# Attention kept in the order of issue on all engines, with each step of a head released by an account of when its operands are ready

## The chip, the cores and the metric

The kernel runs on one core of one Trainium2 chip. The metric is the device time of one execution in microseconds (us). A core has a matrix engine (PE, with its weight loads shown as PEld), a vector engine (DVE), a scalar engine (ACT), a general engine (POOL) and a queue that issues transfers (SP). Each engine works through its own queue in order and waits at an instruction until that instruction's operands are there.

## The reference, cut to what matters

Two layers on 256 tokens of width 1024, in float32. Each layer is a gated feed-forward part, a mixer, and a second feed-forward part. The mixer of layer 0 is differential attention, that of layer 1 is retention. The change touches the attention:

```python
q, k, v = jnp.split(xn @ w_in, 3, axis=-1)            # 8 heads, 2 maps of 64, values of 128
q = _rms(q.reshape(B, T, H, 2, Dh), q_gain) * (Dh ** -0.5)
k = _rms(k.reshape(B, T, H, 2, Dh), k_gain)
...
s = jnp.einsum('bhmqd,bhmkd->bhmqk', qb, k)           # causal, with a slope per head
p = jax.nn.softmax(s + bias[None, :, None], axis=-1)
a = p[:, :, 0] - lmbda * p[:, :, 1]
o = jnp.einsum('bhqk,bhkd->bhqd', a, v)
...
o = _rms(o, subln) * (1.0 - lam_init)
return o.reshape(B, T, H * 2 * Dh) @ w_out
```

## The kernel before, in words

**Products.** Each float32 weight matrix is split into two parts that PE takes at full rate: `hi`, a rounded copy made by ACT, and `lo = raw - hi`, made by DVE. A product is three matmuls of 128 x 512: hi by hi, lo by hi, hi by lo. The class `Weights` loads raw blocks (`load`, six buffers), rounds them (`round`, `remain`) into at most four parts ahead of PE, and hands them out in a planned order (`take`). One part of a projection serves 24 wide matmuls.

**The account.** `Flow` carries an account of time while the program is written out: `flow.now` moves with every matmul (`mm` calls `tick`), and `flow.free` says until when DVE and ACT are taken. `Timed` wraps DVE and ACT and charges every instruction a fixed price and one per column (160 ns and 1.04 ns for DVE, 190 and 0.85 for ACT). Side work is written as generators: `spawn` starts one, `yield n` asks to go on n ns later, and `tick` resumes those that are due. What DVE and ACT have left is given to rounding weights (`paced`).

**The order.** By default a scheduler of the framework, which has its own idea of when an instruction is ready, may put the instructions of an engine in another order than they were issued in. `keep_order` adds an order between successive instructions of each engine. `order_from_here` marks where a kept stretch begins and `order_to_here` closes it. Before the change, stretches are kept from the start to the first `q` projection of attention, from the last chunks of attention's output projection to the first value projection of retention, and from the last chunks of retention's output projection to the end. Between them the scheduler's order holds, but for SP, whose order is kept over the whole program.

**Attention.** `proj_tokens` projects `q`, `k` of heads 0 to 3 (group 0), then of heads 4 to 7 (group 1), into PSUM banks `pj`. `grouped_norm` squares them (`sq`, ACT), sums (`ss`, DVE), takes the power -1/2 (`r`, POOL), scales (`qn`, DVE) and transposes (`ptn`, PE); ACT copies the result to `T_q` or `T_k`. `head` makes for each of its two maps the scores `s` (PE), adds the bias (`sb`, DVE), takes the negative maximum (`nm`, DVE) and the exponential with its sum (`p` and `z`, ACT); then the reciprocal of the sums (`rz`) and the difference of the maps (`att`, DVE), its transposes (`pa`, PE) and their copy (`aT`, ACT). `values` multiplies with `v` into `po`, and `values_norm` norms that into `oT`. The values of both groups are projected after `k` of group 1, and then the output projection `y_dao` runs: two chunks of 24 wide matmuls each that need `oT` of group 0, and two that need group 1. `ffn` is the feed-forward part; its `finish_unit` transposes a gated unit `g` into `hT` through a bank `ptg`.

Of the kernel before, what the change touches and what calls it, by code (L numbers as in the profile page):

```python
# [21 lines left out]
NT = T // P  # L22
# [38 lines left out]
class Flow:  # L61
# [7 lines left out]
    def __init__(self):  # L69
        self.now, self.tasks, self.n = 0.0, [], 0  # L70
        self.urgent, self.casts, self.idle = 0, 0, lambda: None
        self.free = {"DVE": 0.0, "ACT": 0.0}

# [41 lines left out]

    def soon(self, at, by=0):
        return at <= self.now + self.SOON + by


class Timed:  # L120
# [5 lines left out]
    def __getattr__(self, name):  # L126
        issue = getattr(self.engine, name)

        def call(*args, **kw):
            n = max(math.prod(x.shape[1:]) for x in args if hasattr(x, "shape"))  # L130
            self.flow.charge(self.key, self.fixed + self.each * n)
# [220 lines left out]
def trunk_kernel(ctx: ExitStack, tc: tile.TileContext, io, out: bass.AP):  # L352
# [9 lines left out]
    flow = Flow()  # L362
# [119 lines left out]
    def transposes(name, src, n):  # L482
# [3 lines left out]
        flow.now += 115 * n  # L486
        return pt
# [52 lines left out]
    def inv_rms(ss_ap, n, name):  # L540
        r = small.tile([P, n], F32, tag=f"r{n}", name=f"r_{name}")
        nc.gpsimd.tensor_tensor(r, ss_ap, half[:, :n], ALU.pow)
        return r
# [118 lines left out]
    def out_proj(nk, src, coef, name, gain, sums=None):  # L662
# [3 lines left out]
        order_from_here()  # L666
# [7 lines left out]
    def ffn(name, before, sums, next_gain, next_sums=None, last=False):  # L674
# [13 lines left out]
        def finish_unit(j, gs):  # L688
            yield max(g[1] for g in gs) - flow.now + 500
# [9 lines left out]
            split_to(hT[j][:, :, 0, :], hT[j][:, :, 1, :], pt.rearrange("p (i c) -> p i c", c=T))  # L699
            ends[j] = flow.free["DVE"]  # L700
# [117 lines left out]
    def attention(before, next_gain, next_sums):  # L818
# [3 lines left out]
        def grouped_norm(ps, ng, dim, name, margin):  # L822
# [3 lines left out]
            flow.behind("DVE", flow.free["ACT"])  # L826
# [4 lines left out]
            yield flow.through("DVE") + (1900 if ng == 8 else 1200)  # L831
# [7 lines left out]
            yield flow.through("DVE") + margin  # L839
# [23 lines left out]
        def head(g, hh, qT, kT, need, wait, res):  # L863

            yield wait
            yield from all_of(need)
            while flow.through("DVE") > 1500:
                yield 300
            slope = 2.0 ** (-8.0 * (g * 4 + hh + 1) / DA_H)
            z = small.tile([P, 4], F32, tag="z", name=f"z_{g}{hh}")  # L870
            ps_ = []
            for m in range(2):
                name = f"{g}{hh}{m}"
# [8 lines left out]
                flow.now += 650  # L882
                sb = work.tile([P, 384], F32, tag="a", name=f"sb_{name}")
# [3 lines left out]
                for t, cs in enumerate(sides):  # L887
                    vec.tensor_reduce(nm[:, t : t + 1], sb[:, cs], AX.X, ALU.max, negate=True)
                    sca.activation(
# [7 lines left out]
                flow.behind("DVE", flow.free["ACT"] - 700)  # L897
            yield flow.through("DVE", "ACT")
# [11 lines left out]
            yield flow.through("DVE") + 1500  # L910
            pt = transposes(f"pa_{g}{hh}", a, 3)
            if (g, hh // 2) not in res:
                res[g, hh // 2] = blk(f"aT_{g}{hh}", F32, [2, 384])
            sca.copy(res[g, hh // 2][:, hh % 2, :], pt[:, :384])
# [3 lines left out]
        def values(g, v, need, outs):  # L918

            po = [bank(f"po_{g}{t}") for t in range(NT)]  # L920
            for hh in range(4):
                yield from all_of([need[hh]])
                if hh == 0:
# [260 lines left out]
```

## Time and profile before

| | |
|---|---|
| median of three runs | 1066.44 us (1064.53 to 1068.25) |
| the profiled execution | 1065.27 us, its span 1063.5 us |
| PE busy | 1045.8 us, 98% |
| DVE busy | 780.6 us, 73% |
| ACT busy | 589.1 us, 55% |
| POOL busy | 52.2 us, 5% |
| read from memory | 184 GB/s over the span |

The profile is one execution of the program. The span runs from its first to its last instruction; the rest of its time lies around it. A busy time is the sum of an engine's records without overlaps. Records of successive matmuls overlap, so for PE the distance between starts says more than the length of a record. A note such as `[0.40 <-DVE att L132]` says that the engine stood idle for 0.40 us before the instruction and which instruction's end released it. `PEclk` is the share of full clock granted to PE.

### The profile page before, as it was taken

The page shows a single profiled execution, that of the slowest core. Times are in us where ns is not written, and L with a number is a line of the kernel's source. Part 1 is how long each engine was busy: PE and PEld are TensorE (multiplying, and loading weights), DVE is VectorE, ACT ScalarE, POOL GpSimd, SP SyncE. Part 2 cuts the span into 40 slices and gives each one's busy share as a digit, 9 for nine tenths or more (in the row PEclk, how much of TensorE's full clock was granted, in tenths as well). Part 3 has the DMA queues.
Part 4 walks back from the last instruction along what each step waited for, and adds up shares of the span by engine and source line. Part 5 has one row for each costly group of instructions (what it writes and reads, how often), then busy time and mean ns, then how long its engine had stood idle before and what let it go on. Part 6 is the DMA issues. An engine that isn't in the chain of part 4 may idle for free.

```text
span 1063.5 us, 12519 instructions
## 1 busy us (share of the span) xinstructions
PE 1045.8 (98%) x4883; PEld 859.6 (81%) x4883; DVE 780.6 (73%) x751; ACT 589.1 (55%) x657; POOL 52.2 (5%) x62
## 2 busy tenths in 40 slices
PE   8999999999899999999999999999999999999998
PEld 6787888877578888888888888888888888888886
DVE  6687888688767878787787778666556547877883
ACT  7464565656546655655656456555444436565651
POOL 0000000121001000000000000000000000000000
PEclk9999999999899999999999999999999999999999
DMA  9967968364138697869578867664454497597741
GB/s 285 320 202 227 297 203 307 112 242 152 41 118 238 187 268 234 241 237 266 150 238 237 238 214 268 228 232 142 136 166 168 148 283 202 189 265 234 223 159 39
DMA packets 138814, 221.61 MB, mean 208 GB/s; under 512 B 5762, under 2 KB 104834, under 8 KB 135683
## 3 DMA queue, kind: packets, MB, share of 16 engines
q1 hardware_dynamic: 135298, 195.65, 54.8%
q0 software_dynamic: 3456, 25.17, 12.3%
q8 instruction: 38, 0.62, 0.2%
q14 instruction: 22, 0.17, 0.0%
HBM read 194.58 MB, written 1.05 MB: 184 GB/s over the span
## 4 chain that ended last, share of the span: by engine, by line
PE 84%; DMA 5%; DVE 5%; issue 2%; ACT 2%; SPq 1%; POOL 1%; POOLq 0%; DVEq 0%; ACTq 0%
PE b_f L445 19%; PE ps_f L445 16%; PE pj L445 11%; PE y_f1o L445 6%; PE y_f2o L445 6%; PE y_f3o L445 6%; PE pqk L445 4%; PE y_f0o L445 4%; PE y_rto L445 4%; DMA raw<-raw 3%; DVE lo L132 2%; DMA raw<-in_ffn_w_in_dram 2%; PE y_dao L445 2%; PE ptg_f L694 2%; ACT hi L132 1%
## 5 line engine op out<-in xcount | busy, mean ns | idle before, releaser
L132 DVE TENSOR_TENSOR lo<-raw,hi 128x2048 fp32r<-128x2048 f32 (+2 forms) x224 | 491.6, 2211 | 110.1 <-ACT hi L132 108.4
L132 ACT CAST hi<-raw 128x2048 fp32r<-128x2048 f32 (+2 forms) x224 | 412.7, 1851 | 198.0 <-DVE raw L132 99.6
L445 PE MATMUL pj<-hi,xn_f2o 128*128 128x512 f32 x256 | 80.9, 393 | 0.0
L445 PE MATMUL pj<-hi,xn_f0o 128*128 128x512 f32 x192 | 62.3, 402 | 0.0
L445 PEld LDWEIGHTS pj<-hi,xn_f2o 128*128 128x128 f32 x256 | 48.0, 188 | 9.6
L445 PE MATMUL y_f1o<-hi,hT_f 128*128 128x512 f32 x176 | 55.6, 392 | 0.0
L445 PE MATMUL y_f2o<-hi,hT_f 128*128 128x512 f32 x176 | 55.6, 392 | 0.0
L445 PE MATMUL y_f0o<-hi,hT_f 128*128 128x512 f32 x176 | 55.3, 392 | 0.0
L445 PE MATMUL y_f3o<-hi,hT_f 128*128 128x512 f32 x176 | 55.3, 392 | 0.0
L132 DVE TENSOR_TENSOR raw<-raw,raw 128x2048 f32<-128x2048 f32 x24 | 54.8, 2283 | 0.0
L445 PE MATMUL ps_f<-hi,xn_in 128*128 128x512 f32 x160 | 50.6, 394 | 1.1 <-ACT xn_in L132 0.9
L445 PE MATMUL ps_f<-hi,xn_dao 128*128 128x512 f32 x160 | 50.2, 393 | 0.0
L445 PE MATMUL ps_f<-hi,xn_rto 128*128 128x512 f32 x160 | 50.2, 393 | 0.0
L445 PE MATMUL ps_f<-hi,xn_f1o 128*128 128x512 f32 x160 | 50.2, 393 | 0.0
L445 PE MATMUL pj<-lo,xn_f2o 128*128 128x512 f32 x128 | 50.1, 392 | 0.0
L232 POOL DMA_DIRECT2D raw<-raw x24 | 21.0, 876 | 494.7 <-DMA raw<-in_ffn_w_in_dram 302.3
L445 PE MATMUL pqk<-xn_f2o,hi 128*128 128x512 f32 x128 | 44.5, 397 | 0.0
L132 DVE TENSOR_TENSOR hT_f<-ptg_f,hT_f 128x512 fp32r<-128x512 f32 x44 | 30.2, 686 | 19.2 <-ACT hT_f L132 18.8
L445 PEld LDWEIGHTS pj<-hi,xn_f0o 128*128 128x128 f32 x192 | 36.4, 192 | 8.0 <-issue 1.0
L445 PE MATMUL y_rto<-hi,mT 128*128 128x512 f32 x128 | 39.7, 390 | 0.0
L445 PE MATMUL pj<-lo,xn_f0o 128*128 128x512 f32 x96 | 38.7, 403 | 0.0
L445 PEld LDWEIGHTS y_f0o<-hi,hT_f 128*128 128x128 f32 x176 | 33.1, 188 | 6.8
(281 smaller groups left out, 2037.3 us busy)
## 6 DMA issues: line engine op xcount, KB each, us to landing
raw<-in_ffn_w_in_dram SPq DMA_DIRECT2D x168, 512.0 KB, 5.6
raw<-in_ffn_w_out_dram SPq DMA_DIRECT2D x44, 1024.0 KB, 6.6
raw<-raw POOLq DMA_DIRECT2D x24, 1024.0 KB, 8.2
raw<-in_rt_w_in_dram SPq DMA_DIRECT2D x24, 1024.0 KB, 5.9
raw<-in_da_w_in_dram SPq DMA_DIRECT2D x12, 1024.0 KB, 6.1
raw<-in_rt_w_out_dram SPq DMA_DIRECT2D x8, 1024.0 KB, 5.1
raw<-in_da_w_out_dram SPq DMA_DIRECT2D x4, 1024.0 KB, 5.0
raw<-in_ffn_w_in_dram SPq DMA_DIRECT2D x16, 128.0 KB, 3.7
```

The source lines that it names most:

```text
L132: return issue(*args, **kw)
L232: self.nc.gpsimd.dma_start(self.raws[to], self.raws[by], accum_op=ALU.add)
L445: nc.tensor.matmul(ps, lhsT=lhsT, rhs=rhs, start=start, stop=stop, skip_group_check=more)
L694: nc.tensor.transpose(pt[:, at : at + P], gs[t][0][:, i * P : (i + 1) * P], ident)
```

## The change

Attention is put into a kept stretch: `order_to_here` after its first projection goes, and `order_from_here` before the last chunks of an output projection is left only for retention's (`rto`). One stretch now runs from the start to retention's first value projection.

The account learns when each tile is ready. `Timed` moves an engine's account behind the tiles that an instruction reads, notes the end for the tile that it writes, and charges 190 ns more where a sum is accumulated. Transposes, scores and powers note their results too. `flow.until(x)` is the time until x is ready, less 50 ns.

The steps of `grouped_norm`, `head` and `values` yield until their operands are ready, in place of fixed margins. A head begins its scores when the head before has handed out its exponentials (`over`), where before it was started 3000 ns after it, and it begins each map only while DVE has no more than 1200 ns queued. In every feed-forward part `finish_unit` keeps the pacer from rounding weights on ACT in the last 1500 ns before its transposes.

```diff
--- before.py
+++ after.py
@@ -70,6 +70,7 @@
         self.now, self.tasks, self.n = 0.0, [], 0
         self.urgent, self.casts, self.idle = 0, 0, lambda: None
         self.free = {"DVE": 0.0, "ACT": 0.0}
+        self.ready = {}
 
     def spawn(self, gen):
         task = {"gen": gen, "due": self.now, "done": False, "n": self.n}
@@ -113,6 +114,14 @@
 
         return max(0, max(self.free[e] for e in engines) - self.now)
 
+    def made(self, x, at):
+
+        self.ready[x.tensor.name] = at
+
+    def until(self, *xs):
+
+        return max(0, max(self.ready.get(x.tensor.name, 0) for x in xs) - self.now - 50)
+
     def soon(self, at, by=0):
         return at <= self.now + self.SOON + by
 
@@ -127,8 +136,17 @@
         issue = getattr(self.engine, name)
 
         def call(*args, **kw):
-            n = max(math.prod(x.shape[1:]) for x in args if hasattr(x, "shape"))
-            self.flow.charge(self.key, self.fixed + self.each * n)
+            flow = self.flow
+            tiles = [x for x in args if hasattr(x, "tensor")]
+            n = max(math.prod(x.shape[1:]) for x in tiles)
+            reads = tiles[1:] + [x for k, x in kw.items() if hasattr(x, "tensor")]
+            flow.behind(self.key, max([flow.ready.get(x.tensor.name, 0) for x in reads] + [0]))
+            flow.charge(self.key, self.fixed + self.each * n)
+            end = flow.free[self.key]
+            flow.made(tiles[0], end)
+            if "accum_out" in kw:
+                flow.charge(self.key, 190)
+                flow.made(kw["accum_out"], flow.free[self.key])
             return issue(*args, **kw)
 
         return call
@@ -484,6 +502,7 @@
         for j in range(n):
             nc.tensor.transpose(pt[:, j * P : (j + 1) * P], src[:, j * P : (j + 1) * P], ident)
         flow.now += 115 * n
+        flow.made(pt, flow.now + 150)
         return pt
 
     def normed(task, t):
@@ -540,6 +559,7 @@
     def inv_rms(ss_ap, n, name):
         r = small.tile([P, n], F32, tag=f"r{n}", name=f"r_{name}")
         nc.gpsimd.tensor_tensor(r, ss_ap, half[:, :n], ALU.pow)
+        flow.made(r, max(flow.now, flow.ready.get(ss_ap.tensor.name, 0)) + (800, 1200, 1900)[n // 4])
         return r
 
     def new_xn(name):
@@ -663,7 +683,8 @@
         y = OutProj(nk, src, coef, name, gain, sums=sums)
         for c in range(nk // 2 - TAIL):
             y.chunk(c)
-        order_from_here()
+        if name == "rto":
+            order_from_here()
         return y.finish()
 
 
@@ -686,7 +707,10 @@
             return g, flow.free["DVE"]
 
         def finish_unit(j, gs):
-            yield max(g[1] for g in gs) - flow.now + 500
+            wait = max(g[1] for g in gs) - flow.now + 500
+            yield max(0, wait - 1500)
+            flow.casts += 1
+            yield min(wait, 1500)
             pt = bank(f"ptg_{name}{j}")
             for i in range(2):
                 for t in range(NT):
@@ -697,6 +721,7 @@
             flow.now += 300
             hT[j] = blk(f"hT_{name}{j}", F32R, [2, 2, T])
             split_to(hT[j][:, :, 0, :], hT[j][:, :, 1, :], pt.rearrange("p (i c) -> p i c", c=T))
+            flow.casts -= 1
             ends[j] = flow.free["DVE"]
 
         def unit(*js):
@@ -823,12 +848,12 @@
 
             sq = work.tile([P, 512], F32, tag="xs", name=f"sq_{name}", bufs=3)
             sca.activation(sq, ps, AF.Square)
-            flow.behind("DVE", flow.free["ACT"])
+            yield flow.until(sq)
             ss = small.tile([P, ng], F32, tag=f"ss{ng}", name=f"ss_{name}")
             vec.tensor_reduce(ss, sq.rearrange("p (g d) -> p g d", d=dim), AX.X, ALU.add)
             vec.tensor_scalar_add(ss, ss, dim * EPS)
             r = inv_rms(ss, ng, name)
-            yield flow.through("DVE") + (1900 if ng == 8 else 1200)
+            yield flow.until(r)
             qn = work.tile([P, 512], F32, tag="xs", name=f"qn_{name}", bufs=3)
             vec.tensor_tensor(
                 qn.rearrange("p (g d) -> p g d", d=dim),
@@ -836,7 +861,7 @@
                 r.unsqueeze(2).broadcast_to([P, ng, dim]),
                 ALU.mult,
             )
-            yield flow.through("DVE") + margin
+            yield flow.until(qn) + 100
             return transposes(f"ptn_{name}", qn, 4).rearrange("p (j c) -> p j c", c=P)
 
         def heads_norm(t, ps, dst, gcol, name):
@@ -860,16 +885,19 @@
 
         sides = (slice(0, P), slice(P, 384))
 
-        def head(g, hh, qT, kT, need, wait, res):
-
-            yield wait
+        def head(g, hh, qT, kT, need, wait, state, res):
+
+            yield 0
             yield from all_of(need)
-            while flow.through("DVE") > 1500:
-                yield 300
+            while wait is not None and not wait["over"]:
+                yield 200
             slope = 2.0 ** (-8.0 * (g * 4 + hh + 1) / DA_H)
             z = small.tile([P, 4], F32, tag="z", name=f"z_{g}{hh}")
+            yield flow.until(qT, kT)
             ps_ = []
             for m in range(2):
+                while flow.through("DVE") > 1200:
+                    yield 200
                 name = f"{g}{hh}{m}"
                 ms = slice(m * DH, (m + 1) * DH)
                 ps = bank(f"s_{name}")
@@ -880,12 +908,16 @@
                     ps[:, P:384], lhsT=qT[ms, hh, P:T], rhs=kT[ms, hh, :], start=True, stop=True
                 )
                 flow.now += 650
+                flow.made(ps, flow.now + 100)
+                yield flow.until(ps)
                 sb = work.tile([P, 384], F32, tag="a", name=f"sb_{name}")
                 vec.scalar_tensor_tensor(sb, dist, -slope, ps[:, :384], ALU.mult, ALU.add)
                 nm = small.tile([P, 2], F32, tag="nm", name=f"nm_{name}")
                 p = work.tile([P, 384], F32, tag="sb"[m], name=f"p_{name}")
                 for t, cs in enumerate(sides):
                     vec.tensor_reduce(nm[:, t : t + 1], sb[:, cs], AX.X, ALU.max, negate=True)
+                yield flow.until(nm) - 300
+                for t, cs in enumerate(sides):
                     sca.activation(
                         p[:, cs],
                         sb[:, cs],
@@ -894,8 +926,8 @@
                         accum_out=z[:, 2 * m + t : 2 * m + t + 1],
                     )
                 ps_.append(p)
-                flow.behind("DVE", flow.free["ACT"] - 700)
-            yield flow.through("DVE", "ACT")
+            state["over"] = True
+            yield flow.until(z)
             rz = small.tile([P, 4], F32, tag="rz", name=f"rz_{g}{hh}")
             vec.reciprocal(rz, z)
             vec.tensor_scalar(rz[:, 2:4], rz[:, 2:4], nlam, None, ALU.mult)
@@ -907,10 +939,11 @@
                 vec.scalar_tensor_tensor(
                     a[:, cs], ps_[0][:, cs], rz[:, t : t + 1], ps_[1][:, cs], ALU.mult, ALU.add
                 )
-            yield flow.through("DVE") + 1500
+            yield flow.until(a) + 150
             pt = transposes(f"pa_{g}{hh}", a, 3)
             if (g, hh // 2) not in res:
                 res[g, hh // 2] = blk(f"aT_{g}{hh}", F32, [2, 384])
+            yield flow.until(pt)
             sca.copy(res[g, hh // 2][:, hh % 2, :], pt[:, :384])
 
         aTs, oT = {}, {}
@@ -920,8 +953,7 @@
             po = [bank(f"po_{g}{t}") for t in range(NT)]
             for hh in range(4):
                 yield from all_of([need[hh]])
-                if hh == 0:
-                    yield flow.through("ACT") + 1000
+                yield flow.until(aTs[g, hh // 2], v) + 100
                 aT = aTs[g, hh // 2][:, hh % 2, :]
                 hs = slice(hh * P, (hh + 1) * P)
                 for t, cs, vt, first, last in (
@@ -934,9 +966,10 @@
                     )
                 flow.now += 670
                 yield 0
+            for t in range(NT):
+                flow.made(po[t], flow.now + 100)
             norms = [flow.spawn(values_norm(g, t, po[t], outs)) for t in range(NT)]
-            yield 0
-            flow.join(*norms)
+            yield from all_of(norms)
 
         def values_norm(g, t, po, outs):
             pt = yield from grouped_norm(po, 4, 2 * DH, f"o{g}{t}", (2500, 500)[g])
@@ -946,7 +979,7 @@
             flow.behind("DVE", flow.free["ACT"])
             vec.scalar_tensor_tensor(lo, pt, go, hi, ALU.mult, ALU.subtract)
 
-        heads = {}
+        heads, states = {}, []
         wts.reserve(2)
         for g in range(2):
             qT, need = proj_heads(gq, f"q{g}", before if g == 0 else (None, None))
@@ -955,12 +988,15 @@
                 vec.tensor_scalar(
                     nlam, le[:, 1:2], le[:, 0:1], LAM_INIT, ALU.subtract, ALU.subtract
                 )
-                order_to_here()
             kT, more = proj_heads(gk, f"k{g}")
             need += more
-            heads[g] = [
-                flow.spawn(head(g, hh, qT, kT, need, 3000 * hh, aTs)) for hh in range(4)
-            ]
+            heads[g] = []
+            for hh in range(4):
+                states.append({"over": False})
+                wait = states[-2] if len(states) > 1 else None
+                heads[g].append(
+                    flow.spawn(head(g, hh, qT, kT, list(need), wait, states[-1], aTs))
+                )
         tv = []
         for g in range(2):
             v = blk(f"v_{g}", F32, [NT, 512])
```

## Rows read from the trace of the kernel before

**Rows 1.** Windows: length, then PE, PEld, DVE, ACT, POOL busy, PEclk, DMA, GB/s
```profile
0.00:100.00 100.00, 93.25 (x414) 74.13 (x415) 71.18 (x75) 60.24 (x70) 5.83 (x12) 1.00 0.91 272
198.40:323.20 124.80, 118.18 (x586) 93.21 (x585) 92.92 (x170) 72.11 (x132) 21.11 (x15) 0.96 0.41 133
271.20:290.50 19.30, 14.36 (x62) 9.99 (x61) 14.85 (x46) 9.91 (x36) 2.01 (x2) 0.74 0.13 43
340.00:1000.00 660.00, 659.99 (x3089) 548.42 (x3089) 483.54 (x400) 362.18 (x364) 22.44 (x31) 1.00 0.71 218
```

**Rows 2.** Chain of work that ended last: start us, length us, what
```profile
258.74 0.43 PE s L876 x4
...
305.16 15.68 PE y_dao L445 x69
```

**Rows 3.** Windows of PE's `pj` (two) and `y_dao` (one) alone, as rows 1
```profile
271.20:290.50 19.30, 7.92 (x26) 0.74 0.13 43
277.00:295.40 18.40, 7.54 (x24) 0.72 0.00 0
...
295.30:304.90 9.60, 5.20 (x20) 1.00 0.39 111
```

**Rows 4.** Timeline of PE: start us, length us, line, instruction, idle before and releaser
```profile
257.54 0.30 PE L485 MATMUL pa<-ident,att 128*128 128x128 f32 x1 [0.59 <-DVE att L132]
...
275.70 0.30 PE L485 MATMUL pa<-ident,att 128*128 128x128 f32 x1 [0.40 <-DVE att L132]
...
278.71 0.30 PE L485 MATMUL pa<-ident,att 128*128 128x128 f32 x1 [1.78 <-DVE att L132]
...
287.68 0.45 PE L485 MATMUL pa<-ident,att 128*128 128x128 f32 x1 [2.76 <-DVE att L132]
...
303.53 0.66 PE L485 MATMUL ptn_o<-ident,qn_o 128*128 128x128 f32 x4 [0.99 <-DVE qn_o L132]
```

**Rows 5.** Timeline of DVE in attention, columns as rows 4
```profile
232.86 1.01 DVE L132 SCALAR_TENSOR_TENSOR sb<-dist,s 128x384 f32<-128x384 f32 x2
...
258.44 0.69 DVE L132 TENSOR_TENSOR qn_k<-pj,r_k 128x512 f32<-128x512 f32 x1 [0.65 <-POOL r_k L542]
259.63 0.56 DVE L132 SCALAR_TENSOR_TENSOR sb<-dist,s 128x384 f32<-128x384 f32 x1 [0.50 <-PE s L879]
...
262.66 0.18 DVE L132 RECIPROCAL rz<-z 128x4 f32<-128x4 f32 x1 [0.72 <-ACT p L132]
...
263.60 0.74 DVE L132 SCALAR_TENSOR_TENSOR att<-p,rz,p 128x128 f32<-128x128 f32 x2
...
287.85 1.12 DVE L132 TENSOR_REDUCE nm<-sb 128x1 f32<-128x128 f32 x4
...
294.17 2.29 DVE L132 TENSOR_TENSOR lo<-raw,hi 128x2048 fp32r<-128x2048 f32 x1 [2.37 <-ACT hi L132]
...
305.92 0.75 DVE L132 SCALAR_TENSOR_TENSOR oT<-ptn_o,go,oT 128x512 fp32r<-128x512 f32 x1 [0.22 <-ACT oT L132]
```

**Rows 6.** Tile `ptg_f`, 0 to 100 us and whole: idle before it, us, times
```profile
  DVE g_f L132: 6.7, 4
```

**Rows 7.** Timeline of ACT in attention, columns as rows 4
```profile
230.68 0.69 ACT L132 ACTIVATE T_k<-ptn_k,gk 128x512 f32<-128x512 f32 x1 [1.67 <-PE ptn_k L485]
...
266.21 0.67 ACT L132 ACTIVATE T_k<-ptn_k,gk 128x512 f32<-128x512 f32 x1
...
294.04 0.47 ACT L132 COPY aT<-pa 128x384 f32<-128x384 f32 x1
...
299.68 0.60 ACT L132 ACTIVATE sq_o<-po 128x512 f32<-128x512 f32 x1 [1.98 <-PE po L932]
```

**Rows 8.** Waits of PE and PEld, 198 to 324 us: us in total, times, longest
```profile
PE pa L485 <- DVE att L132: 5.5, 4, 2.8
...
PEld pa L485 <- issue: 7.3, 6, 3.5
...
PEld pa L485 <- ACT v L132: 1.0, 1, 1.0
```

## The prediction, made before the change was run

> **What bounds the kernel now.** I read the page first: TensorE (PE) is busy for 98% of the span. That share is too coarse here, because a matmul's record covers more than its slot, so I cut the span into stages [rows 1]. From 340 to 1000 us PE is never idle, while DVE has 27% and ACT 45% to spare. There the kernel is bound by PE alone, and an edit that only moves DVE or ACT work can gain nothing. The attention stage, 198.4 to 323.2 us, is different: in 271.2 to 290.5 us PE shows 14.36 us of 19.30, the DMA engines stand almost still (0.13), and the mean granted clock is 0.74, so part of the stretch ran at 1.2 instead of 2.4 GHz after PE had stood idle in it [rows 1].
>
> What a stretch should have cost I take from two prices: 69 wide matmuls in a row took 15.68 us, so 0.227 us each, and four records of a head's scores took 0.43 us, so 0.108 us each [rows 2]. In 271.2 to 290.5 us there are 62 PE records [rows 1], 26 of them wide [rows 3]: 26 x 0.227 + 36 x 0.108 = 9.8 us; some eight changes between narrow and wide matmuls cost about 0.1 us each, so 10.6 us. Lost: 8.7 us. The timeline of PE shows where: before the transposes `pa` at 275.70, 278.71 and 287.68 [rows 4]. All three wait for `att` from DVE, and wide matmuls stand right behind them in the queue: 24 of `v1`'s start only after 277 [rows 3], 48 more belong to the first two chunks of `y_dao`, and only those after them need the second group of heads. So PE waits with 72 x 0.227 = 16 us of work behind the wait that does not need it. That is a fault of order, not of speed. The same at 303.53, where `ptn_o` stands in front of `y_dao` (0.99 us) [rows 4], and at 257.54, where PE stood 0.59 us. Together 8.7 + 1.0 + 0.6 = **10.3 us**: no ordering of attention can give more than that.
>
> **The change part by part.** *Order of issue kept on all engines in attention* (two marks moved). It adds and removes no instruction. It gives the queue its order from the kernel's own account, not from the scheduler's. The account holds PE to a step of 7 + 512/2.4 = 220 ns against 227 measured [rows 2], and charges a head's DVE steps more than they take: `sb` 160 + 1.04 x 384 = 559 ns against 1.01 us for two [rows 5]. So a product of DVE is as a rule ready before the place in PE's queue that was given to its reader. I take the 10.3 us back in full, and charge for what this order can lose:
>
> *Gates.* Twelve norms, eight `att`, sixteen score steps and eight heads of `values` are now handed out 100 to 150 ns after (or up to 50 ns before) the account has the operand: 44 gates on PE, with everything queued behind each. The nearest row is the 44 groups `ptg_f`, gated with 500 ns: PE stood before them four times, 6.7 us, all within the first 100 us [rows 6], where the DMA share was 0.91 [rows 1]; after that it never waited for their operand. Bounds: 0 and 6.7 us. The DMA share in attention is far below that [rows 1], nearer to the later groups, but the margins are a third of theirs: I take 2 us. The old gates had 500 to 2500 ns more; these are what the shorter chain pays with.
>
> *Chain of the heads.* A head's scores now begin when the one before has its exponentials handed out (`over`), and the second map's after the first's. A head whose scores met no weight work took from 258.7 us to the reciprocal at 262.66, 4.0 us [rows 2, 5]. To this come parts of the last head's `rz` to `att` that do not fit into gaps (about 0.7 of the 1.7 us from 262.66 to 264.34 [rows 5]), and the `lo` of the weights, 2.29 us each [rows 5], one per 24 wide matmuls, so one in about 7 us with the narrow ones. T = 4.0 + 0.7 + 2.29 x T/7 gives T = 7.0 us per head. The first starts at 231.4 (end of `T_k` [rows 7]). The first of group 1 needs `T_k` of `k1`: `qn_k` ended at 259.1 [rows 5], the copy of its transposes came only at 266.21 [rows 7]; gated at 100 ns they give `T_k` at about 262, and four heads end at 290. Before, it took from 288.7 (300 ns ahead of the last maximum) to 294.5 until the last `aT` [rows 5, 7]: 5.8 us. The last head's six narrow records of `po` take 6 x 0.108 = 0.7, the norm from `sq_o` at 299.68 to the end of `oT` at 306.67 took 7.0 for two halves [rows 5, 7], of which the first is enough to go on, so 6.5, and 0.3 for the poll: 7.5. End: 290 + 5.8 + 7.5 = 303.3 us.
>
> PE needs that `oT` at its 49th `y_dao`. Before, 20 of them were done at 304.9 [rows 3], so it came there at 304.9 + 28 x 0.227 = 311.3; with 10.3 us given back, at 301.0. So a stall of 2.3 us remains, and this is what is late next: DVE's chain of the last heads. Each 0.1 us on T costs 0.4 to 0.8 us once this cover is gone.
>
> *Accounts* (`made`, `until`, reads in `Timed`, 190 ns for an accumulator's read). They also move weight work in the feed-forward parts. Cover: PE without a gap from 340 us on [rows 1]. If it were gone, the four waits of 6.7 us [rows 6] are what could move, 1.7 us each; I take 0, and as ends one of them gone or added, -2 and +2 us.
>
> *`finish_unit` holds casts back for 1.5 us* before its transposes, 44 times. Hidden by ACT's idle 40% and by up to four parts rounded ahead; without the cover each could make a part 1.5 us late, and nothing shows a part late from 340 us on. Taken at 0. A gain is excluded there, since PE has no gap to give back.
>
> *Queues passed.* SP's order was kept over the whole kernel already. On POOL only the twelve powers `r_q`, `r_k` and `r_o` stand in this stage, each behind its own `ss`, and in the order in which their readers want them. Neither costs.
>
> Sum: -10.3 + 2 (gates) + 2.3 (chain) = -6 us. The profiled execution took 1065.27 us (span 1063.5 and 1.8 around it); it becomes 1059.3. The median of the three runs shown is 1.2 us above it: **1060.4 us**.
>
> **The rivals.**
> 1. *The chain is covered in full.* If the DVE steps, which are shorter than their charges, let T come to 6.4 us or less, `oT` is ready by 301 and only gates remain: -8 to -10.3, about 1057 us. For it: two `sb` are charged 1.12 us and take 1.01, and the small reductions are charged 160 ns each on top of their columns. Against it: a `lo` that slips in costs 2.29 us whatever the charges [rows 5].
> 2. *The chain becomes the bound, and the kernel slower.* Price: in group 0 before, the first `sb` of heads 0 and 3 stand 26.8 us apart, 8.9 us per head [rows 5]. If the new order keeps that spacing, the end comes at 231.4 + 8 x 8.9 + 13.3 = 315.9, a stall of 14.9 us: with the gates' 2, less the 10.3, +6.6, so about 1073 us. It decides from 231.4 + 8T + 13.3 = 309.3, T = 8.1 us: two `lo` in each head instead of one (4.7 + 4.6 = 9.3) do it. Against it: the new code waits for the scores of the head before alone, and lets its `rz` to `att` run beside the next scores.
> 3. *The waits at `pa` are not the order's.* If a `pa` waited for a PSUM bank, the order of issue leaves it as it is, and 0 to 2 us come back: 1065 us. The trace has 1.0 us before `pa` that ACT's copy of `v` ended, which reads another bank; 5.5 us on PE are `att`'s own, and 7.3 us of the weight loads before `pa` have no cause named [rows 8]. The Trainium skill, Perfetto Trace Analysis, section Identifying Performance Opportunities, says that the same gap repeated on the engine that should be full can mean too few buffers for the next tile; by that rule this case, and not the order, would be the whole story. The trace agrees for 1.0 us of it and not for the 5.5.
>
> **How the numbers follow.** A difference of less than 0.3%, 3.2 us, cannot be told from no change. Forecast (-3.2 to -8): 0.48. Rival 1 (-8 to -12.3): 0.17. Rival 3, or a chain with T near 8 (within 3.2 us): 0.18. Rival 2: 0.17. So faster 0.65, same 0.18, slower 0.17. The range goes from all 10.3 us with the accounts' 2 (1066.4 - 12.3 = 1054) to 1069, a little above no change, which leaves out the larger part of rival 2.
>
> **What would show it.** PE in 271 to 290 us with no gap over 0.5 us before `pa`, and granted clock 1.00 there; `y_dao` ending near 317 instead of 323 us; the one wait left before the 49th `y_dao`, for `oT`; spacing of the heads' first `sb` near 7 us. A spacing over 8.1, or a wait of more than 8 us before `oT`'s first reader, makes the forecast wrong. New gaps in 340 to 1000 us would mean that the accounts or the held casts cost what I took at 0.

## The result and the profile after

The changed kernel takes 1074.80 us in the median against 1066.67 for the kernel before, 1.0069 times as long (95% interval 1.0052 to 1.0087). The forecast was 1060.4, in a range of 1054 to 1069. It was wrong in sign; rival 2, the chain of the heads as the bound, had 1073. That this lies near is in part luck: rival 2 had a stall of 14.9 us and nothing for the scores, and the trace has 12.0 and 6.6.

The profiled execution has a span of 1071.6 us, 8.1 more than before. By the start of the first `pj`, the end of the last `y_dao` and the end of the last `y_f3o` in both traces it divides so: up to attention -1.4 us (198.4 before, 197.0 after), attention +7.5 (124.9 before, 132.4 after), behind it +2.0 (736.1 before, 738.1 after).

The windows of the kernel after answer [rows 1] (columns: stretch, its length, then busy time and count of PE, PEld, DVE, ACT and POOL, granted clock of PE, DMA share, GB/s):

```profile
198.40:323.20 124.80, 117.95 (x551) 90.18 (x550) 92.47 (x162) 68.72 (x125) 22.48 (x14) 0.95 0.41 131
271.20:290.50 19.30, 19.30 (x103) 15.22 (x102) 15.55 (x31) 11.48 (x26) 1.98 (x2) 1.00 0.18 56
340.00:1000.00 660.00, 658.73 (x3078) 545.89 (x3077) 483.91 (x400) 362.59 (x366) 21.61 (x30) 1.00 0.70 216
```

The stretch that held the forecast's gain, 271.2 to 290.5 us, is now full: 19.30 of 19.30 us and clock 1.00, where before it was 14.36 and 0.74. The waits of [rows 4] before `pa` are gone. They came back in another place. PE's timeline of the kernel after, end of attention (start, length, operation; in brackets the idle time just before it and who ended it):

```profile
302.05 0.59 PE L907 MATMUL s<-T_k,T_q 64*128 64x256 f32 x2
302.58 0.55 PE L503 MATMUL pa<-ident,att 128*128 128x128 f32 x3
303.94 0.94 PE L964 MATMUL po<-v,aT 128*128 128x128 f32 x6 [0.81 <-ACT aT L150]
307.29 0.45 PE L503 MATMUL pa<-ident,att 128*128 128x128 f32 x1 [2.42 <-DVE att L150]
307.98 0.69 PE L503 MATMUL pa<-ident,att 128*128 128x128 f32 x2 [0.25 <-DVE att L150]
309.24 1.65 PE L964 MATMUL po<-v,aT 128*128 128x128 f32 x6 [0.57 <-ACT aT L150]
313.49 2.10 PE L503 MATMUL ptn_o<-ident,qn_o 128*128 128x128 f32 x8 [2.60 <-DVE qn_o L150]
315.44 1.58 PE L463 MATMUL y_dao<-hi,oT 128*128 128x512 f32 x2
316.82 0.63 PE L463 MATMUL y_dao<-lo,oT 128*128 128x512 f32 x1
317.25 1.05 PE L463 MATMUL y_dao<-hi,oT 128*128 128x512 f32 x2
318.11 0.63 PE L463 MATMUL y_dao<-lo,oT 128*128 128x512 f32 x1
318.53 0.85 PE L463 MATMUL y_dao<-hi,oT 128*128 128x512 f32 x2
319.23 0.39 PE L463 MATMUL y_dao<-lo,oT 128*128 128x512 f32 x1
```

From 302.58 to 315.44 PE does 26 narrow matmuls, 2.8 us at 0.108 each, in 12.9: 10.0 us lost. Of these 6.65 are idle time, the five notes in brackets added up; the other 3.4 are narrow matmuls that took longer than their price, most of them at the lower clock. No wide matmul stands between, since all 336 that don't need the second group (288 `pj`, 48 `y_dao`) were issued ahead of the last head's second scores. Then eight wide matmuls, 315.44 to 319.23, take 3.8 us instead of 8 x 0.227 = 1.8: 2.0 more, at the lower clock. This tail costs 12 us.

Why the last head is so late, DVE's timeline of the kernel after shows; it answers [rows 5]. The first two rows are the first `sb` of the first head and of the fifth, the rest is from the seventh head's first map on:

```profile
230.87 0.56 DVE L150 SCALAR_TENSOR_TENSOR sb<-dist,s 128x384 f32<-128x384 f32 x1 [1.84 <-PE s L907]
...
265.93 0.55 DVE L150 SCALAR_TENSOR_TENSOR sb<-dist,s 128x384 f32<-128x384 f32 x1 [1.07 <-ACT p L150]
...
284.66 0.55 DVE L150 SCALAR_TENSOR_TENSOR sb<-dist,s 128x384 f32<-128x384 f32 x1 [0.24 <-PE s L907]
285.25 0.61 DVE L150 TENSOR_REDUCE nm<-sb 128x1 f32<-128x128 f32 x2
286.91 0.75 DVE L150 SCALAR_TENSOR_TENSOR oT<-ptn_o,go,oT 128x512 fp32r<-128x512 f32 x1 [1.06 <-ACT oT L150]
287.58 2.28 DVE L150 TENSOR_TENSOR lo<-raw,hi 128x2048 fp32r<-128x2048 f32 x1
289.78 0.17 DVE L150 RECIPROCAL rz<-z 128x4 f32<-128x4 f32 x1
...
291.22 0.48 DVE L150 SCALAR_TENSOR_TENSOR att<-p,rz,p 128x256 f32<-128x256 f32 x1
291.62 2.29 DVE L150 TENSOR_TENSOR lo<-raw,hi 128x2048 fp32r<-128x2048 f32 x1
294.67 0.56 DVE L150 SCALAR_TENSOR_TENSOR sb<-dist,s 128x384 f32<-128x384 f32 x1 [0.76 <-PE s L907]
295.26 0.61 DVE L150 TENSOR_REDUCE nm<-sb 128x1 f32<-128x128 f32 x2
297.32 0.55 DVE L150 SCALAR_TENSOR_TENSOR sb<-dist,s 128x384 f32<-128x384 f32 x1 [1.45 <-PE s L907]
```

The first map of the seventh head has its maximum at 285.9; the bias of its second map starts at 294.67. Between lie two `lo` and the steps of the head before. The new code makes the second map's scores wait until the account has DVE free to within 1.2 us (`flow.through("DVE") > 1200`), and each `lo` moves that point on. It also issues them only after the first map's exponentials are handed out. In the mean of the eight heads the bias of the second map starts 5.3 us behind that of the first; before, it came 0.5 to 1.6 us behind it (for one head 259.63 [rows 5] and 260.75). The first `sb` of the eight heads stand at 230.87 (the first) to 297.32 us (the last): 66.45 / 7 = 9.5 us per head, and within the second group, from 265.93 on, 31.39 / 3 = 10.5. The forecast had 7.0, and 8.1 as the point from which the chain is the bound.

A third cost stands on PE. The scores of one map alone, in the kernel after:

```profile
236.13 0.48 PE L904 MATMUL s<-T_k,T_q 64*128 64x128 f32 x2
236.45 0.59 PE L907 MATMUL s<-T_k,T_q 64*128 64x256 f32 x2
236.97 0.50 PE L463 MATMUL pj<-hi,xn_f0o 128*128 128x512 f32 x1
```

and those of both maps of a head, in the kernel before:

```profile
258.67 0.50 PE L876 MATMUL s<-T_k,T_q 64*128 64x128 f32 x4
259.00 0.61 PE L879 MATMUL s<-T_k,T_q 64*128 64x256 f32 x4
259.53 0.74 PE L445 MATMUL pj<-hi,xn_f0o 128*128 128x512 f32 x2
```

Four records alone hold PE for 0.84 us (236.13 to 236.97), eight together for 0.86 (258.67 to 259.53). The two maps lie in different halves of the 128 rows, and their matmuls ran at the same time. The change issues every map by itself: 16 x 0.84 - 8 x 0.86 = 6.6 us more on PE.

Together in attention: -10.3 (waits gone) + 0.4 (one gate, before `ptn_q` at 217.73: 0.20 us idle, 0.59 from the start before it in place of 0.227) + 6.6 + 12.0 = +8.7, against 7.5 in the trace; the parts are good to about 1 us each.

### The profile page after: what moved, and what is told of

The parts are those of the page before. It is cut to its first block, busy times and chain, and to the rows that moved or that the text cites. A ratio compares the mean times of both kernels' runs of the same rounds, so it can differ in the third digit from the quotient of the medians.

```text
span 1071.6 us, 12499 instructions
## 1 busy us (share of the span) xinstructions
PE 1053.8 (98%) x4883; PEld 862.2 (80%) x4883; DVE 785.6 (73%) x751; ACT 589.2 (55%) x657; POOL 54.2 (5%) x62
## 4 chain that ended last, share of the span: by engine, by line
PE 88%; DMA 4%; DVE 3%; ACT 2%; issue 1%; SPq 1%; POOL 0%; POOLq 0%; ACTq 0%; DVEq 0%
PE b_f L463 19%; PE ps_f L463 17%; PE pj L463 14%; PE y_f1o L463 6%; PE y_f3o L463 6%; PE y_f2o L463 6%; PE pqk L463 4%; PE y_f0o L463 4%; PE y_rto L463 4%; DMA raw<-raw 2%; PE y_dao L463 2%; PE ptg_f L718 2%; DVE lo L150 1%; ACT hi L150 1%; DMA raw<-in_ffn_w_in_dram 1%
## 5 line engine op out<-in xcount | busy, mean ns | idle before, releaser
L463 PEld LDWEIGHTS y_f3o<-hi,hT_f 128*128 128x128 f32 x176 | 33.1, 188 | 6.8
L463 PEld LDWEIGHTS y_f2o<-hi,hT_f 128*128 128x128 f32 x176 | 33.0, 188 | 6.8
## 6 DMA issues: line engine op xcount, KB each, us to landing
raw<-in_ffn_w_in_dram SPq DMA_DIRECT2D x16, 128.0 KB, 3.6
```

The lines of the kernel that those rows point to most:

```text
L463: nc.tensor.matmul(ps, lhsT=lhsT, rhs=rhs, start=start, stop=stop, skip_group_check=more)
```

## The experiments

Three theories: *order* (to keep the order of issue in attention is itself the loss), *handing out* (the account hands out the heads too late, so that the last one stalls PE), *scores* (maps issued apart cost PE time). The 95% interval of the ratio to the kernel before stands behind each time. For small differences the length of attention in the profiled execution says more than the time: what lies ahead of attention took from 196.5 to 200.4 us in these executions, by no pattern that follows the edits.

**The two halves of the change.** *a1* is the kernel before with the marks of the kept order alone; *a2* is the kernel after with the marks back.

```diff
-        order_from_here()                 # a1, in out_proj; a2 the reverse
+        if name == "rto":
+            order_from_here()
 ...
-                order_to_here()
```

> The kernel before with the two marks moved alone: order of issue kept in attention, old account and old margins. Three theories of the 8 us. Order: the order of issue by itself is worse than the scheduler's, because PE is held to places that DVE cannot keep; then this kernel is slower than before by 5 us or more (1072 or more) and PE stands before `pa` and `po` as before or longer. Handing out: order alone is harmless and the new steps of a head (gates and the wait for the head before) make the chain of heads late; then it lies within 3 us of before (1064 to 1070), with the last group of heads ending before the second chunk of the output projection. Scores: the loss is PE time of scores that are no longer issued in pairs; the two maps are issued together here, so a pair takes about 0.43 us per map and the time is near before.

> The changed kernel with the two marks where they were: new account and new steps of a head, but the scheduler orders attention. Order theory: back near before (1064 to 1069). Handing-out theory: the issue order is only a priority for the scheduler, which lets ready work pass, so most of the tail stall (10 us of idle PE from 302.6 to 315.4 and about 2 us at half clock after it) goes: 1063 to 1070. Scores theory: the scheduler may bring the two maps together again or not; where a map stands alone, its four records take 0.85 us, where both stand together both take 0.86, and the time follows their number.

a1: 1069.31 us (1.0020 to 1.0038). a2: 1074.38 us (1.0044 to 1.0078), the whole loss, where two of the theories had expected 1070 or less: the scheduler did not bring the heads forward, and the last scores stand behind all 336 wide matmuls here too. The stretch of the waits, 271.2 to 290.5 us, first in a1, then in a2:

```profile
271.20:290.50 19.30, 15.17 (x69) 10.85 (x70) 16.64 (x42) 7.60 (x25) 2.07 (x2) 0.82 0.18 56
```

```profile
271.20:290.50 19.30, 19.30 (x102) 14.96 (x102) 15.46 (x35) 11.62 (x26) 1.98 (x2) 1.00 0.27 85
```

With the order kept and the old account the waits before `pa` stay; with the new account and the scheduler's order they are gone and the tail stands whole. The longest of a1's five waits before `pa`, 4.8 us together, and its own tail, then a2's:

```profile
274.85 0.45 PE L485 MATMUL pa<-ident,att 128*128 128x128 f32 x1 [2.30 <-DVE att L132]
...
302.53 2.10 PE L485 MATMUL ptn_o<-ident,qn_o 128*128 128x128 f32 x8 [4.82 <-DVE qn_o L132]
```

```profile
305.00 0.94 PE L963 MATMUL po<-v,aT 128*128 128x128 f32 x6 [0.81 <-ACT aT L150]
308.35 0.45 PE L503 MATMUL pa<-ident,att 128*128 128x128 f32 x1 [2.42 <-DVE att L150]
...
314.55 2.10 PE L503 MATMUL ptn_o<-ident,qn_o 128*128 128x128 f32 x8 [2.60 <-DVE qn_o L150]
```

So the order of issue explains 2 to 4 us with the old account (a1's 1.0020 to 1.0038), and nothing on top of the new account (1074.38 and 1074.80). The theory *order* falls, and with it the forecast's reason for the gain: the new times of handing out removed the waits, not the kept order.

**Gate and pairs.** *a5* takes the gate on DVE out; *a6* also issues both maps' scores together; *a3* issues them together behind one gate per head.

```diff
             for m in range(2):
-                while flow.through("DVE") > 1200:      # a5, a6; a3 keeps it, ahead of the loop
-                    yield 200
                 ps = bank(f"s_{name}")
                 ...
+                banks.append(ps)                       # a6, a3
+            for m in range(2):
+                ps = banks[m]
                 yield flow.until(ps)
```

> The changed kernel without the wait until DVE has no more than 1200 ns queued, which stands before each of a head's two maps. In the order of PE the last scores then stand after 309 wide matmuls of the stage instead of 336 of the 336 that do not need group 1: 27 places, 6.1 us earlier. Handing-out theory: the stall of PE before the last `po` and the last norm shrinks by 4 to 6 us, so 1069 to 1071, and the spacing of the heads falls from 9.5 to about 8.3 us. Scores theory: each map still stands alone, PE's work is the same, and the time stays within 2 us of the changed kernel (1073 to 1077). Order theory: no change either.

> As the kernel without the gate, and both maps' scores of a head are issued one behind the other before either map goes on. In PE's order the last scores stand after 295 wide matmuls (41 places, 9.3 us earlier than in the changed kernel). Scores theory: eight pairs of 0.86 us in place of sixteen single maps of 0.85 give 6.7 us back, so 1067 to 1069 whether or not the chain is shorter. Handing-out theory: freed PE time is worth nothing while the chain of heads sets the end; what counts is that the chain ends earlier, by 5 to 8 us against the changed kernel: 1066 to 1070, with PE still waiting before the last `po`.

> The changed kernel with both maps' scores of a head issued one behind the other, the 1200 ns gate kept, once per head. PE has 6.7 us less to do, but in its order the last scores still stand behind all 336 wide matmuls that do not need group 1, as in the changed kernel. Scores theory: 6 to 7 us back, 1067 to 1069. Handing-out theory: the last head's chain behind the filler is as long as before, so PE reaches it earlier and the freed work shows at the end only because that chain begins at a place in PE's queue and not at a time: the tail stall of 12 us stays whole, and the gain is the 6.7 us less what the waits of the chain take back, 1068 to 1073.

| | maps apart | maps together |
|---|---|---|
| with the gate | 1074.80 (after) | 1069.84 (a3: 1.0025 to 1.0053) |
| without it | 1072.75 (a5: 1.0038 to 1.0068) | 1063.33 (a6: 0.9959 to 0.9983) |

The gate alone is worth 2.0 us, the pairs alone 5.0, both 11.5; the gate's 2.0 is hardly clear of the intervals (1.0052 to 1.0087 for after), but attention is shorter by 2.7 us in a5 too (132.4 after, 128.0 in a3, 129.7 in a5, 120.5 in a6). a5 missed its 1069 to 1071, and a6 came out below both of its ranges. Counted in wide matmuls in the order of issue, the last scores stand behind all 336 in after and in a3, behind 309 in a5, 295 in a6 (264 in the kernel before). Why both edits give more than the sum is seen in the tails. Above the price of their matmuls, to the point where the wide ones run at 0.227 us again, they lose 12.0 us in after, 14.1 in a3, 9.2 in a5 and 8.3 in a6. With the gate a part of the PE time that the pairs give back is lost again: in a3 PE comes to the tail 5.8 us earlier than in after (296.8 and 302.6), the last `att` only 2.8 (305.1 and 307.9), and PE stands another 1.4 us before 291. Without the gate nothing of it is lost. The tail of a6:

```profile
301.07 0.94 PE L966 MATMUL po<-v,aT 128*128 128x128 f32 x6 [1.76 <-ACT aT L150]
305.63 2.09 PE L503 MATMUL ptn_o<-ident,qn_o 128*128 128x128 f32 x8 [3.62 <-DVE qn_o L150]
```

Both theories, *handing out* and *scores*, hold, and some 5 us of idle time are still left in this tail.

**The steps behind the scores, and the haste of the weights.** *a7* is a6 with the biases and maxima of both maps in one piece, and a pair charged 860 instead of 1300 ns. *c1* is the kernel after with the weights in less haste during attention; *c2* is a7 with it; *e1* is c2 with less haste only from the second group on. The loops of a7 that put the two maps' steps in one piece are not shown.

```diff
-        return 2000 * max(0, 3 - (len(self.parts) - len(self.rounded) - self.taken))
+        return 2000 * max(0, self.want - (len(self.parts) - len(self.rounded) - self.taken))
 ...
+        wts.want = 1                           # c1, c2: attention, back to 3 in the second half of y_dao
+            wts.want = 3 if g == 0 else 1      # e1, per group
 ...
-                flow.now += 650                # a7, c2, e1
+                flow.now += 430
```

> On top of pairs without the gate: bias and maxima of both maps go to DVE in one piece, so that no weight remainder (`lo`, 2.28 us) slips in between the two maps, and the account charges a pair of scores 860 ns in place of 1300. If the chain of the heads sets the end (handing-out theory), one `lo` less in each head of group 1 brings the last `att` 2 to 4 us earlier: 1059 to 1062. If the pairs were all (scores theory), it stays within 1.5 us of the 1063.3 of pairs without the gate.

> The changed kernel as it was, gates and single maps included; only the pacer's haste is lowered within attention, so that a weight remainder is put on a busy DVE only when no rounded part is left ahead of PE, where before it was put there when fewer than three were. In PE's order the last scores come after 304 wide matmuls instead of 336 (7.3 us earlier). If weight remainders on DVE are what stretches the heads, the tail stall of 12 us shrinks by 6 to 8: 1066 to 1070. If single maps are the loss, PE has the same 6.8 us of extra work and the time stays at 1073 to 1076. If weights come late instead, PE stands before `lo` and the time is above 1075.

> Pairs, both maps' DVE steps in one piece, no gate, and less haste. In PE's order everything of group 1 stands ahead of the 337th wide matmul (last `po` after 288, last norm after 320), so the chain has cover. Handing-out theory with cover: the stage costs PE work and gates alone, 10.3 us less than before with 2 us kept for gates: 1057 to 1060. If remainders of weights come late by it, PE stands before `lo`: 1061 to 1066.

> As the kernel with pairs and less haste, but haste is lowered only once the second group is projected, since the lowered haste made PE wait 3 us before the first transposes of `q` and `k` and 1.5 us for a `lo` in the first group. If those waits were haste's, 3 to 4 us go: 1056 to 1058, with everything of group 1 still ahead of the 337th wide matmul. If the waits come from the first powers on POOL, it stays at 1060 to 1061.

a7: 1064.84 us (0.9961 to 0.9986), no gain over a6. c1: 1074.32 (1.0041 to 1.0080), none over after. c2: 1060.62 (0.9907 to 0.9953), 4.2 under a7. e1: 1057.45 (0.9897 to 0.9927), faster than both kernels, 9.6 us under the before of its runs. a7's tail stays at two waits, as in a6. c1 shows that haste is not the cause by itself: the heads come earlier in PE's order (last scores behind 304), but the maps stay apart, 5.2 us from a `y_dao` at 310.24 to the next matmul remain, and some 3 us go to waits between the projections. In c2 and e1 the last scores stand behind 252 and 247 wide matmuls and the last norm behind 320, so nothing of the second group is left when the 337th needs it. In e1 attention lasts from 196.9 to 312.6, 115.7 us: 9.2 less than before. Of the 3.2 us that e1's time lies under c2's, only 1.4 are attention's (117.1 in c2); the rest lies ahead of it, where the edit does not reach, so its expectation of 3 to 4 us is borne out in part.

The spacing of the heads' first `sb` within the second group, whose last head the tail waits for, falls step by step: 10.5 us in after, 10.1 in a3, 8.3 in a5, 6.8 in a6, 6.1 in a7, 4.2 in c2. The first of these four heads starts at 265.8 to 269.6 in all of them, so the first group's spacing hardly matters to the end. Of the 6.3 us per head the gate is worth 2.2, the maps together 1.5, their DVE steps in one piece 0.7 and the weights' haste 1.9, in this order of the edits.

The stretch 198.4 to 323.2 of e1, whose attention ends at 312.6, and the longest waits of PE in its attention (engine line, waited for, us in total, times, longest):

```profile
198.40:323.20 124.80, 122.22 (x629) 97.20 (x628) 100.97 (x179) 78.20 (x140) 25.23 (x16) 1.00 0.44 145
```

```profile
PE pj L464 <- DVE lo L150: 1.3, 1, 1.3
PE pa L504 <- DVE att L150: 0.3, 1, 0.3
```

**Price of maps apart by itself, and the account.** *c3* was meant to set the maps of c2 apart. But `Flow.step` adds the yielded time to a `now` read before the generator ran, and so the second map was due at once: the maps stayed in eight groups of eight. What the edit did was to charge 1720 ns for a pair instead of 860. *c5* sets the maps of the first group apart, with two wide matmuls between.

```diff
-                flow.now += 430               # c3
+                flow.now += 860
+                if g == 0:                    # c5
+                    yield 680
```

> As the one with pairs and less haste, but the two maps of a head are scored 250 ns apart by the account, so that a wide matmul stands between them. Since the chain has cover in that kernel, the difference of the two is the price of scoring the maps singly: by the records 16 x 0.85 - 8 x 0.86 = 6.7 us, so 6 to 8 us above it. If PE's extra time is hidden by waits anyway, the two agree within 2 us.

> The kernel with pairs, one piece of DVE work per head and less haste, but in the four heads of group 0 two wide matmuls stand between the scores of the two maps. The last norm stands 325 wide matmuls into the stage in place of 320, so the cover of the end is about the same. Scores theory by the records: 4 x (2 x 0.85 - 0.86) = 3.4 us above the 1060.6 of that kernel, 1063 to 1065. If PE hides a single map's slower scores, within 1.5 us of it.

c3: 1065.88 us (0.9972 to 0.9997), 5.3 above c2, by the charge alone: the last `po` now stands behind 324 wide matmuls and the tail is back:

```profile
307.56 1.97 PE L504 MATMUL ptn_o<-ident,qn_o 128*128 128x128 f32 x8 [4.69 <-DVE qn_o L150]
```

It says nothing on maps apart. c5: 1061.81 (0.9939 to 0.9969), 1.2 above c2, where the records of four heads price it at 4 x (1.68 - 0.86) = 3.3. But in the profiled executions, whose difference is 0.6, attention takes 117.1 us in c2 and 120.2 in c5, 3.1 more, while what lies ahead of it, where the edit does not reach, takes 2.6 less (199.1 and 196.5). c2 also has a 1.07 us wait for a `lo` before a `pj` at 260.14 that c5 has not. So, by one execution of each, PE does not hide the price where there is slack: in attention it is about what the records say. For all eight heads they say 6.6 us; a5 to a6 gave 9.4, with the shorter chain in it.

**The hold in `finish_unit`.** *b2* is the kernel after without it.

```diff
             yield max(0, wait - 1500)
-            flow.casts += 1
             yield min(wait, 1500)
 ...
-            flow.casts -= 1
```

> The changed kernel without the hold on weight casts in the last 1500 ns before a unit's transposes; attention as in the change. If the hold costs nothing, as I took it, the time stays within 1.5 us of the 1074.8 of the changed kernel; if it is behind the 2 us that the changed kernel loses after attention (a wait of 1.5 us for `lo` at 341.7 among them), 1072 to 1073; if it helps the feed-forward parts, above 1076.

b2: 1080.95 us (1.0114 to 1.0144), 6.1 above after. PE now waits in the feed-forward parts, where neither before nor after does; PE's timeline of b2, one of several such places:

```profile
593.45 0.50 PE L463 MATMUL y_f2o<-hi,hT_f 128*128 128x512 f32 x1 [0.54 <-ACT hT_f L150]
594.17 0.50 PE L463 MATMUL y_f2o<-hi,hT_f 128*128 128x512 f32 x1 [0.22 <-DVE hT_f L150]
```

From the end of `y_dao` to the end of `y_f3o` it is 736.1 us before, 742.6 in b2, 738.1 after. With the marks alone (a1) it is 736.1, and with the marks back (a2) 738.1, so the order has no part in it. So behind attention the other edits, of which the accounts are the ones that reach there, cost 6.5 us and the hold gives 4.5 back. Idle time of PE behind 345 us explains 1.9 of these 4.5; the rest shows as no idle time. (The rest of the 6.1 lies ahead of attention, where the two executions also differ in their first weights; it is not put down to the hold.) The accounts alone were not run. A kernel without the wait for the head before (`over`) was not tried.

## Why the prediction was wrong, point by point

- *"That is a fault of order, not of speed."* The size held, the cause did not. The waits went, and e1 takes 9.2 us from attention. But a1 keeps the order and has the waits; a2 leaves the scheduler its order and has none. What fails is the premise that an account puts the reader of a DVE product late enough. In the order of the old account (a1) PE reaches `pa` before the end of `att`, in spite of a margin of 1500 ns; the new account puts it later. This error did not turn the sign, since the change has both.
- *Gates, 2 us.* The row [rows 6] was misread: its 6.7 us count the same two waits once on PE and once on its weight loads. The waits of the kernel before, 0 to 100 us:

```profile
PE ptg_f L694 <- DVE g_f L132: 3.0, 2, 1.5
```

```profile
PEld ptg_f L694 <- DVE g_f L132: 3.8, 2, 1.9
```

  So the upper bound was 3.0 us and not 6.7, and one wait 1.5. One short wait, 0.20 us of idle time, is all that a gate cost PE ahead of the tail. The gate between the maps has its price in the lateness that it gives to what it hands out: 2.0 us of time in a5.
- *Chain of the heads, T = 7.0, stall 2.3 us.* This is the step that failed, and the term that turned the sign: T measured 9.5, and the stall of 2.3 is a tail of 12. PE had its last independent work behind it at 302.6 us (forecast 301.0), but its 49th `y_dao` came at 315.4 (forecast 303.3). The forecast took the cost of a head from heads whose maps ran back to back [rows 2, 5], with one `lo` in about 7 us. It noted that "the second map's after the first's" and gave it no price; that distance is 5.3 us in place of 0.5 to 1.6. Rival 2 named the outcome, but not quite the mechanism: eight `lo` lie in the seven spacings, and two in only three of them, so its condition, two `lo` in each head, was not met. The forecast's argument against it, "the new code waits for the scores of the head before alone", overlooked the gate and the wait between the maps.
- *Scores, no term in the sum.* The forecast read four records in 0.43 us [rows 2] and gave no price to a map that is issued by itself. But 0.43 is half of a pair, and 0.84 is a map by itself. The sum lacked 6.6 us that no chain explains. The trace of before held the sign of it: the records of the two maps start in pairs 13 ns apart (258.670 and 258.683, for one), which one map after the other could not do.
- *Accounts and hold, each 0, "a gain is excluded there".* The bounds of -2 and +2 held for the sum: +2.0 behind attention. That is luck: it is +6.5 and -4.5. An idle margin on ACT and a full PE say nothing on an edit when another one takes that cover away.
- *Queues passed.* POOL also has `r_f0o` and `r_dao` at the ends of this stage, besides the twelve powers; the sum does not change by them.
- *Rival 3, PSUM banks.* The Trainium skill, Perfetto Trace Analysis, section Identifying Performance Opportunities, puts a repeated gap on the engine that should be full down to missing buffers as a possibility. Here the trace disagrees: with the same banks the gaps between 271.2 and 290.5 us are gone, by another time of handing out.
- *What would show it.* PE full from 271 to 290 us, right. The spacing over 8.1 came, 9.5, and `y_dao` ended at 329.4 where about 317 was forecast. The "wait of more than 8 us before `oT`'s first reader" did not come as one wait: the idle time lies in five pieces, 6.65 us together, the last of them before `ptn_o`. One `lo` behind attention now costs PE 1.15 us of idle time, before 343.26, where it was 0.25 before 336.30; a1 has 0.25 and a2 1.19, so it came with the new account and not with the order; why it grew is open. e1 has the same wait (1.14).

## What to carry to other kernels

Where a program hands out its own work, a gate costs little where PE stands at it and much in the place that the work gets: follow the last item of the chain to the count of independent matmuls that are left behind it. A wait that vanishes in the middle may stand whole at the end, where nothing is left to put beside it. Before two steps are taken apart, look whether their price was that of a pair, and price edits that lean on the same slack together.

## What the hardware showed that was not expected

Two matmuls that contract 64 rows each, one in the lower and one in the upper half of the array, and that are issued back to back, run at the same time: eight records in 0.86 us, against 0.84 for four of one half alone. The Trainium skill, TensorEngine Tiling (Array Packing), section Key Properties, says that tiles of the array are independent and that different ones can load weights and multiply in parallel; the trace agrees, for a program that asked for no tiling by name.

Within the tail the clock that PE was granted fell to 0.50, the 1.2 GHz level, and stayed there until 319.0 us, with PE at work without a gap from 313.49 on. It fell at about 305.4, while PE stood idle for the 2.42 us before 307.29, after 0.81 us of idle time before 303.94. Windows of the kernel after, columns as above:

```profile
302.50:305.30 2.80, 1.56 (x10) 1.06 (x9) 2.64 (x5) 2.27 (x6) 0.00 (x0) 1.00 1.03 325
305.40:319.00 13.60, 8.29 (x25) 5.73 (x26) 6.94 (x15) 3.05 (x5) 2.94 (x3) 0.50 0.39 79
315.50:319.10 3.60, 3.60 (x9) 2.52 (x9) 1.43 (x2) 0.69 (x1) 0.00 (x0) 0.51 0.00 0
319.50:323.00 3.50, 3.50 (x17) 2.89 (x16) 1.38 (x2) 0.72 (x2) 0.00 (x0) 1.00 0.00 0
```

Nine records against seventeen in like stretches of wide matmuls: this is where 2.0 us went on top of the 10.0 ahead of them, and it is most of the 3.4 by which the narrow matmuls of the tail outran their price. In e1, without such a tail, the whole attention stage has 1.00.
